# One layer kernel with three mixers: decay rates moved within the first stage, and attention's products with the values issued for two key blocks and both heads together

## The chip, the cores and the metric

The kernel runs on one core of a Trainium2 chip. A core has five engines with a queue of instructions each: TensorE (PE in the profile; its weight loads are PEld), VectorE (DVE), ScalarE (ACT), GpSimd (POOL) and SyncE (SP, which only issues transfers here). The metric is the device time of one execution in microseconds. The kernel before takes 876.51 us, the median of three runs (876.1 to 877.89).

## The reference, cut to what matters

Two layers work on 512 tokens of width 1024, all in 32-bit floats. Each layer normalises its input, projects it, runs three mixers side by side on the projection, and adds their gated and projected outputs to its input.

```python
for l in range(DEPTH):                      # DEPTH = 2
    xn = rms_norm(h, ln_g[l])
    proj = xn @ w_in[l]
    u_a, z_a, u_b, z_b, q_lat, kv_lat, k_rope, z_c = jnp.split(proj, pts, axis=-1)
    y_a = rwkv7_mix(u_a, ...)               # a recurrence over tokens, 8 heads of 64
    y_b = rms_norm(rglru_mix(u_b, ..., lru_lam[l]), lru_out_g[l])
    y_c = rms_norm(mla_mix(q_lat, kv_lat, k_rope, ...), mla_out_g[l])
    y = concatenate([y_a * silu(z_a), y_b * silu(z_b), y_c * silu(z_c)])
    h = h + y @ w_out[l]
return rms_norm(h, final_g)
```

Two pieces matter here. In `rglru_mix` the decay of the gated recurrence is `log_a = -8 * gate_r * softplus(-lam)`. The factor `softplus(-lam)` depends on the parameter `lam` alone (512 numbers in each layer). In `mla_mix` each of 8 heads computes causal attention: scores, a softmax over the keys up to the query, and the product of the probabilities with the values, in blocks of 128 queries and keys.

```python
s = jnp.where(k_pos[None, :] <= q_pos[:, None], s, -jnp.inf)
p = jax.nn.softmax(s, axis=-1).astype(v.dtype)
return jnp.einsum('bhqk,bkhd->bqhd', p, v)
```

## The kernel before, in words

Tiles have 128 partitions. The large projections are made of three products each (`mm3`, L230 to L233), with weight and activation split into a high and a low part; ScalarE makes the high part of a weight (L140 through `copy`), GpSimd or VectorE the low part (L227).

A layer runs in stages. Orders written by hand name the steps of the first stages: ORD1 for the recurrence's inputs, then ORD2 and ORD3. In ORD1, `M` is the projection and token mix of a head pair (L498 is VectorE's share), `L` the low-rank products with a sigmoid on ScalarE (L540, L541), `C` the chain that forms decay, keys and their scaling (L552 to L584, mostly on VectorE, with exponentials on ScalarE and products on GpSimd), `O` a bonus term (L592 to L595), `P` the products of keys with queries and their masks (L610 on TensorE, L613 on VectorE, then transposes L628), and `U` the values (L637). Four head pairs are numbered 0 to 3. ORD2 begins with gates (`G`), the remaining `U` and `P`, and the substitution `X` (L728 to L749), a long run of VectorE instructions behind which the corner products L758 to L773 stand.

The program order gives each instruction its priority. A planner in the framework then fixes each engine's queue ahead of time: it takes the ready instruction of the highest priority by its own costs, adds the waits that the data need, and the hardware works each queue in order. Activation functions that need a table are chained in program order on ScalarE (`act`, L132).

`decay_rates` (L260 to L278) computes the softplus of both layers once, in layer one, after ORD1. It is one exponential on ScalarE and 25 VectorE instructions on 128 x 8 numbers, among them a polynomial in a loop (L271 to L273). Its results, `sp8` and `nsp8`, are read by the gated recurrence (L694, L701).

Attention works on head pairs too. `score_steps` gives 8 steps for each pair: a score product (L1037) into one of four accumulators, a mask and a maximum on VectorE (L1038, L1039), the exponential with its sum on ScalarE (L1041, by way of L137), and the scaling on VectorE (L1044). `heads` then takes the four key blocks one after the other: for both heads it transposes the probabilities (L1056), copies them to SBUF on ScalarE (L1058, shown as L140), runs fill steps, and multiplies by the values (L1062). The stationary operand there is 128 x 64, and each product is two passes on TensorE. Head 0 writes partitions 0 to 63 of `ot`, head 1 partitions 64 to 127. The fill steps come from the string QH: `s` is a score step of the next head pair, `u` a step of the output projection (L405 is its sum on VectorE).

## Time and profile before

| What | Value |
| --- | --- |
| Median of three runs | 876.51 us (876.1 to 877.89) |
| Profiled execution | 874.73 us, its span 873.0 us |
| Mean granted TensorE clock | 0.973 |
| TensorE busy | 810.8 us, 93% of the span |
| VectorE busy | 578.5 us, 66% |
| ScalarE busy | 494.3 us, 57% |
| GpSimd busy | 336.5 us, 39% |

In the profile a group of instructions is named by line, engine and operation, with the tile written, an arrow and the tiles read. In a timeline the first number is the start in microseconds from the begin of the span and the second the time until the last of the merged instructions ended; a bracket gives the idle time before the first and what ended it. Since matmuls are pipelined, their times overlap, and the distance from start to start is what one costs. A line of `copy`, `act` or `mm3` stands for all who call it.

### The profile page before, as it was taken

The numbers are of one execution on the slowest core, as the hardware profiler recorded it, in microseconds if no ns is written. First come the engines' busy times: TensorE is split into PE (matmuls) and PEld (weight loads), VectorE is DVE, ScalarE is ACT, GpSimd is POOL, SyncE is SP. The second block draws the span as 40 slices with busy tenths as digits, with TensorE's granted clock in tenths as the row PEclk, the third lists the DMA queues.
The fourth block names the chain that finished last, engine by engine and source line by source line (L and its number), as shares of the span: only waits on it lengthen the run. The fifth ranks groups of instructions, "written<-read, shape, count | busy, mean of one in ns | idle before, by whom it ended". The sixth has DMA issues, their size and how long they took to land.

```text
span 873.0 us, 14713 instructions
## 1 busy us (share of the span) xinstructions
PE 810.8 (93%) x5440; PEld 621.4 (71%) x5440; DVE 578.5 (66%) x1176; ACT 494.3 (57%) x980; POOL 336.5 (39%) x303
## 2 busy tenths in 40 slices
PE   3999997998989988999989999999989998899995
PEld 2878886876768866655778788888756886665574
DVE  5678777843656795974484766786265777677636
ACT  5667874457454535564466677844645445465635
POOL 2355554634343342010534655665243423310223
PEclk9999997999899999999989999999999999999998
DMA  6322232420212365222653222333010224731354
GB/s 217 115 73 71 72 103 84 139 74 13 56 39 72 106 221 182 73 68 98 206 195 97 73 93 88 100 107 115 27 42 23 65 86 154 227 114 49 108 168 159
DMA packets 49753, 91.05 MB, mean 104 GB/s; under 512 B 5520, under 2 KB 8336, under 8 KB 49680
## 3 DMA queue, kind: packets, MB, share of 16 engines
q1 hardware_dynamic: 49104, 89.05, 31.7%
q10 hardware_dynamic: 576, 1.05, 0.3%
q8 instruction: 43, 0.70, 0.3%
q14 instruction: 30, 0.25, 0.1%
HBM read 73.30 MB, written 16.78 MB: 103 GB/s over the span
## 4 chain that ended last, share of the span: by engine, by line
PE 69%; DVE 14%; DMA 5%; ACT 5%; issue 4%; POOL 2%; SPq 0%; ACTq 0%; DVEq 0%; POOLq 0%
PE acc L231 15%; PE acc L233 15%; PE acc L232 15%; PE acc L1037 4%; PE ck L1062 3%; PE ps L1056 3%; PE ps L688 2%; PE ck L829 2%; ACT g L137 2%; DMA dr<-hp 2%; DMA g<-dr 1%; POOL g L703 1%; PE ps L628 1%; PE ps L610 1%; PE ck L788 1%
## 5 line engine op out<-in xcount | busy, mean ns | idle before, releaser
L227 POOL TENSOR_TENSOR wL<-wr,wH 128x512 fp32r<-128x512 f32 (+1 forms) x130 | 176.8, 1365 | 291.8 <-ACT wH L140 271.3
L140 ACT ACTIVATE wH<-wr 128x512 fp32r<-128x512 f32 (+1 forms) x192 | 118.7, 622 | 135.7 <-PE acc L232 77.5
L231 PE MATMUL acc<-xH,wH 128*128 128x512 f32 (+1 forms) x496 | 193.0, 390 | 0.0
L233 PE MATMUL acc<-xH,wL 128*128 128x512 f32 (+1 forms) x496 | 192.0, 387 | 0.0
L232 PE MATMUL acc<-xL,wH 128*128 128x512 f32 (+1 forms) x496 | 190.4, 384 | 0.5 <-DVE xL L305 0.4
L231 PEld LDWEIGHTS acc<-xH,wH 128*128 128x128 f32 x496 | 95.5, 193 | 20.8 <-issue 3.2
L232 PEld LDWEIGHTS acc<-xL,wH 128*128 128x128 f32 x496 | 95.7, 193 | 17.9 <-DVE xL L305 1.2
L233 PEld LDWEIGHTS acc<-xH,wL 128*128 128x128 f32 x496 | 95.5, 192 | 17.8
L231 PE MATMUL acc<-wH,c 128*128 128x512 f32 x192 | 81.9, 426 | 4.3 <-DVE hp L427 4.3
L227 DVE TENSOR_TENSOR wL<-wr,wH 128x512 fp32r<-128x512 f32 (+1 forms) x62 | 51.5, 830 | 48.7 <-ACT wH L140 48.6
L232 PE MATMUL acc<-wL,c 128*128 128x512 f32 x192 | 76.8, 400 | 0.4 <-DVE wL L227 0.4
L233 PE MATMUL acc<-wH,c 128*128 128x512 f32 x192 | 76.3, 399 | 0.0
L140 ACT ACTIVATE UV<-ps 128x512 f32<-128x512 f32 (+4 forms) x88 | 39.0, 477 | 38.0 <-PE ps L1056 30.6
L231 PEld LDWEIGHTS acc<-wH,c 128*128 128x128 f32 x192 | 36.3, 189 | 16.1 <-DVE hp L427 3.2
L137 ACT ACTIVATE g<-g 128x512 f32<-128x512 f32 (+1 forms) x58 | 36.5, 628 | 17.5 <-DVE g L706 15.6
L137 ACT ACTIVATE c<-acc,sm 128x128 f32<-128x128 f32 (+3 forms) x64 | 33.6, 527 | 18.7 <-DVE sm L1039 18.5
L233 PEld LDWEIGHTS acc<-wH,c 128*128 128x128 f32 x192 | 36.3, 189 | 8.6 <-issue 1.0
L140 ACT ACTIVATE c<-g 128x512 fp32r<-128x512 f32 (+1 forms) x40 | 24.3, 628 | 31.9 <-DVE g L960 26.4
L232 PEld LDWEIGHTS acc<-wL,c 128*128 128x128 f32 x192 | 36.5, 190 | 8.2 <-issue 1.4
L1037 PE MATMUL acc<-am,am 128*128 128x128 f32 (+3 forms) x128 | 41.5, 445 | 0.8 <-ACT c L137 0.8
L368 POOL TENSOR_TENSOR g<-g,g 128x512 f32<-128x512 f32 x24 | 33.4, 1394 | 12.6 <-ACT g L137 12.6
L135 ACT ACT_TABLE_LOAD x29 | 37.2, 1283 | 1.2 <-PEq L1189 0.7
(218 smaller groups left out, 1604.5 us busy)
## 6 DMA issues: line engine op xcount, KB each, us to landing
wr<-in_wc_dram SPq DMA_DIRECT2D x116, 256.0 KB, 2.7
wr<-in_wo_dram SPq DMA_DIRECT2D x48, 256.0 KB, 3.5
hp<-dr SPq DMA_DIRECT2D x40, 256.0 KB, 3.1
dr<-hp SPq DMA_DIRECT2D x32, 256.0 KB, 2.8
dr<-g SPq DMA_DIRECT2D x16, 256.0 KB, 2.3
g<-dr SPq DMA_DIRECT2D x16, 256.0 KB, 3.6
wr<-in_wl_dram SPq DMA_DIRECT2D x16, 208.0 KB, 2.4
c<-in_x_dram SPq DMA_DIRECT2D x8, 256.0 KB, 6.5
```

Source lines behind the costliest of these rows:

```text
L135: chained(A.preload_act_table_set(SETS[st]))
L137: chained(A.activation(out=out, in_=in_, func=func, **kw))
L140: i = A.activation(out=out, in_=in_, func=AF.Copy, **kw)
L227: (V if wn[0] % wmod[0] == 0 else G).tensor_tensor(out=L, in0=raw, in1=f(H), op=ALU.subtract)
L231: PE.matmul(o, a[0], b[0], start=start, stop=False)
L232: PE.matmul(o, a[0], b[1], start=False, stop=False)
L233: PE.matmul(o, a[1], b[0], start=False, stop=stop)
L368: G.tensor_tensor(out=z, in0=z, in1=s, op=ALU.mult)
L688: PE.matmul(o[hr, :], gw[hr, w, j, :], xc[hr, :], start=True, stop=True)
L1037: PE.matmul(o[:, 0:n], qT[:, hd, qt * 128:n], K2[:, p, e, 0:n], start=True, stop=True)
L1056: PE.transpose(o[:, (qt - kt) * 128:(qt - kt + 1) * 128], Pm[p][e, qt][:, kt * 128:(kt + 1) * 128], ident)
L1062: PE.matmul(ot[e * 64:(e + 1) * 64, kt * 128:T], Vt[:, kt, 2 * p + e, :], pts[e][:, 0:n], start=(kt == 0), stop=(kt == 3))
```

## The change

There are two parts. First, `decay_rates` becomes a step `D` of ORD1, behind the low-rank products `L0` and `L1` and ahead of the first chain `C0`, in layer one only. Its polynomial is also written with fused instructions, which add a constant and multiply in one: 18 VectorE instructions stand in place of 25.

Second, in `heads` the products with the values are issued after each second key block. The group holds both heads of the earlier block and both heads of the later one. Its first product gets an added dependency on the last of the copies of the later block. The fill steps keep their places, behind each block's copies.

```diff
-    ORD1 = "M0 L0 L1 C0 M1 C1 P0 L2 O0 M2 U1 O1 C2 U2 P1 L3 M3 C3 U0 P2 O2"
+    ORD1 = "M0 L0 L1 D0 C0 M1 C1 P0 L2 O0 M2 U1 O1 C2 U2 P1 L3 M3 C3 U0 P2 O2"
...
+    SYNC = mybir.DependencyInfo(mybir.DependencyClass.Sync, mybir.DependencyReason.DATA)
...
-        V.tensor_scalar(out=l3, in0=l2, scalar1=1.0 / 17.0, scalar2=1.0 / 15.0, op0=ALU.mult, op1=ALU.add)
-        for n in (13, 11, 9, 7, 5, 3, 1):
-            V.tensor_tensor(out=l3, in0=l3, in1=l2, op=ALU.mult)
-            V.tensor_scalar(out=l3, in0=l3, scalar1=1.0 / n, scalar2=None, op0=ALU.add)
-        V.tensor_tensor(out=l3, in0=l3, in1=l1, op=ALU.mult)
+        V.tensor_scalar(out=l3, in0=l2, scalar1=1.0 / 17.0, scalar2=None, op0=ALU.mult)
+        for n in (15, 13, 11, 9, 7, 5, 3):
+            V.scalar_tensor_tensor(out=l3, in0=l3, scalar=1.0 / n, in1=l2, op0=ALU.add, op1=ALU.mult)
+        V.scalar_tensor_tensor(out=l3, in0=l3, scalar=1.0, in1=l1, op0=ALU.add, op1=ALU.mult)
...
-        steps = {"L": low_rank, "M": mixes, "C": chain, "O": bonus_term, "P": products, "U": values}
+        steps = {"D": lambda _: decay_rates() if l == 0 else None, "L": low_rank, "M": mixes, "C": chain, "O": bonus_term, "P": products, "U": values}
...
-        if l == 0:
-            decay_rates()
...
-                pts = []
                 for e in range(2):
                     o = ps()
                     for qt in range(kt, 4):
                         PE.transpose(...)
-                    pt = PT[:, 2 * (kt % 2) + e, :]
-                    copy(pt[:, 0:n], o[:, 0:n])
-                    pts.append(pt)
+                    last_pt = copy(PT[:, 2 * (kt % 2) + e, 0:n], o[:, 0:n])
                 fill[kt]()
-                for e in range(2):
-                    PE.matmul(ot[e * 64:(e + 1) * 64, kt * 128:T], Vt[:, kt, 2 * p + e, :], pts[e][:, 0:n], start=(kt == 0), stop=(kt == 3))
+                if kt % 2 == 0:
+                    continue
+                for k2 in (kt - 1, kt):
+                    for e in range(2):
+                        i = PE.matmul(ot[e * 64:(e + 1) * 64, k2 * 128:T], Vt[:, k2, 2 * p + e, :], PT[:, 2 * (k2 % 2) + e, 0:(4 - k2) * 128],
+                                      start=(k2 == 0), stop=(k2 == 3))
+                        if k2 < kt and e == 0:
+                            tc.add_manual_dep(i.ins, last_pt.name, SYNC, reason="one group")
```

## The prediction

> **What bounds the kernel now.** I read the page first, then the chain of waits, then windows and timelines of the two places that the edits touch. TensorE is busy nearly all the time and carries most of the chain, so a change counts by what it does to TensorE's queue: its idle stretches, its clock, and the length of its own instructions.

> ```profile
> span 873.0 us, 14713 instructions
> ...
> PE 810.8 (93%) x5440; PEld 621.4 (71%) x5440; DVE 578.5 (66%) x1176; ACT 494.3 (57%) x980; POOL 336.5 (39%) x303
> ...
> PE 69%; DVE 14%; DMA 5%; ACT 5%; issue 4%; POOL 2%; SPq 0%; ACTq 0%; DVEq 0%; POOLq 0%
> ```

> The profiled execution took 874.73 us, 1.78 us below the median of the runs (876.51). The sum is made against 874.73 and 1.8 is added at the end.

> Both layers run the same stages, and only layer one has the decay rates. So layer two serves as a measurement of layer one without them. The chain of waits gives two marks in each layer: a group of the key-value products and the first corner product after the substitution.

> ```profile
> 94.45 1.16 PE ps L610 x8
> ...
> 180.68 1.91 PE ck L758 x64
> ...
> 524.86 1.16 PE ps L610 x8
> ...
> 602.86 1.91 PE ck L758 x64
> ```

> Layer one takes 180.68 - 94.45 = 86.23 us, layer two 602.86 - 524.86 = 78.00: layer one is 8.2 us longer over the same work. The windows show where (columns: busy time and count of TensorE, weight loads, VectorE, ScalarE, GpSimd, then the granted clock, the DMA share and GB/s):

> ```profile
> 134.10:139.30 5.20, 0.23 (x3) 0.04 (x1) 4.79 (x16) 0.27 (x1) 2.23 (x2) 0.67 0.63 200
> 139.30:146.20 6.90, 6.88 (x23) 5.73 (x24) 2.57 (x4) 3.78 (x6) 0.00 (x0) 0.51 0.00 1
> ```

> TensorE stands still for 5 us while VectorE runs 16 instructions, and then works 6.9 us at a granted clock of 0.51. The idle time costs 5.2, the clock 6.9 x (1 - 0.51) = 3.4; together 8.6, near the 8.2 of the marks. In layer two:

> ```profile
> 564.50:569.70 5.20, 5.20 (x31) 4.28 (x31) 2.61 (x5) 3.98 (x8) 1.82 (x2) 1.00 0.58 186
> ```

> TensorE is full in the same 5.2 us and the clock is 1.00. What VectorE does in layer one's gap, and who waits (timelines of VectorE and TensorE):

> ```profile
> 131.30 1.25 DVE L273 TENSOR_SCALAR sm<-sm 128x8 f32<-128x8 f32 x1
> ...
> 136.40 0.17 DVE L272 TENSOR_TENSOR sm<-sm,sm 128x8 f32<-128x8 f32 x1
> ...
> 138.58 0.68 DVE L613 TENSOR_TENSOR am<-ps,C 128x512 f32<-128x512 f32 x1
> ```
> ```profile
> 139.32 1.11 PE L628 MATMUL ps<-C,c 128*128 128x128 f32 x4 [4.99 <-DVE am L613]
> ```

> The decay polynomial (L272, L273 and what follows) stands in VectorE's queue ahead of the mask products L613 of the third head pair; TensorE waits 4.99 us for them.

> **The change part by part: the decay rates.** The chain has 25 VectorE instructions before and 18 after (14 instructions of the loop become 7, the rest as before). Two of the 18 read only the inputs, which leaves 16 in a row behind the exponential. Moved behind layer one's first two low-rank products, they are no longer ahead of L613. What is late next there is nothing that layer two's windows show, so I take the whole 8.2 as gained. No DMA is issued by this step, and no table load is added: the exponential's table is loaded at that place anyway, before the first chain's exponential.

> Their new place costs something. ScalarE runs the exponential behind this table load, and VectorE has a hole there (timelines of ScalarE, VectorE and GpSimd):

> ```profile
> 49.45 1.28 ACT L135 ACT_TABLE_LOAD   x1
> ```
> ```profile
> 53.63 0.82 DVE L567 TENSOR_TENSOR c<-g 128x512 f32<-128x512 f32 x1 [3.05 <-ACT g L137]
> ```
> ```profile
> 51.45 1.20 POOL L579 TENSOR_TENSOR c<-g,g 128x512 f32<-128x512 f32 x1 [3.74 <-ACT g L137]
> ...
> 54.20 1.40 POOL L227 TENSOR_TENSOR wL<-wr,wH 128x512 fp32r<-128x512 f32 x1 [0.29 <-ACT wH L140]
> ```

> Lower bound: 16 x 0.17 = 2.7 us inside a hole of 3.05, so 0; they only add work, so there is no gain below nothing. Upper bound: the first of the loop's instructions show durations of 1.25 beside 0.17. From 131.30 to 136.40 there are five of them in 5.1 us. GpSimd worked through that stretch until its last instruction ended at 136.33, and from then on the same instruction took 0.17:

> ```profile
> 135.07 1.26 POOL L368 TENSOR_TENSOR g<-g,g 128x512 f32<-128x512 f32 x1
> ```

> At the new place GpSimd is busy from 51.45 to 55.60 almost without a break. About 2 instructions get through before 51.45, 5 until 55.60, and the other 9 at 0.2 end near 57.4: L567 and the first chain behind it start 3.8 us late. Queued behind them on VectorE are L567 to L592 and the mask products of the first head pair, for which TensorE waits. How much of a delay reaches TensorE is read from this window:

> ```profile
> 54.00:68.00 14.00, 13.05 (x71) 10.37 (x70) 12.44 (x16) 7.34 (x15) 9.29 (x10) 1.00 0.23 76
> ```

> VectorE has 14.00 - 12.44 = 1.6 us idle in it, so 3.8 - 1.6 = 2.2 us get through. Bounds 0 and 3.8; I take 2.2, since five equal instructions of this kernel beside a busy GpSimd are the nearest row. Net of this edit: 8.2 - 2.2 = 6.0 us (4.4 to 8.2).

> [...]

> **The change part by part: attention's products with the values.** Before, the products of one key block (two heads, each in two passes) follow that block's transposes; after, two blocks and both heads stand together, and the first waits for the last of the four copies. TensorE's timeline:

> ```profile
> 367.99 0.87 PE L1062 MATMUL ck<-UV 128*64 128x384 f32 x4
> 368.79 0.66 PE L1056 MATMUL ps<-C,c 128*128 128x128 f32 x4
> ...
> 371.13 0.40 PE L233 MATMUL acc<-wH,c 128*128 128x512 f32 x1
> 371.45 0.65 PE L1062 MATMUL ck<-UV 128*64 128x256 f32 x4
> 372.04 0.44 PE L1056 MATMUL ps<-C,c 128*128 128x128 f32 x2
> ...
> 372.54 0.40 PE L232 MATMUL acc<-wL,c 128*128 128x512 f32 x1
> 372.78 0.40 PE L233 MATMUL acc<-wH,c 128*128 128x512 f32 x1
> ...
> 376.06 1.07 PE L1062 MATMUL ck<-UV 128*64 128x512 f32 x2
> 377.07 0.70 PE L1037 MATMUL acc<-am,am 128*128 128x256 f32 x2
> 377.70 1.07 PE L1062 MATMUL ck<-UV 128*64 128x512 f32 x2
> ...
> 397.88 0.86 PE L1062 MATMUL ck<-UV 128*64 128x384 f32 x2
> 398.67 0.50 PE L231 MATMUL acc<-wH,c 128*128 128x512 f32 x1
> ```

> Read from start to next start: a pair of both heads (x4) takes 0.59 at 256 columns and 0.80 at 384, and one head alone (x2) takes 0.79 at 384 and 1.01 at 512. So the second head is free when it stands beside the first, each 128 columns cost 0.21, and 0.16 is left over (0.59 - 2 x 0.21) that is paid once at the end of each group. On the way in, 371.13 to 371.45 is 0.32, where 372.54 to 372.78 is 0.24: 0.08 more, also once for each group.

> Merging: 4 head pairs x 4 blocks x 2 layers make 32 groups into 16. Saved: 16 x (0.16 + 0.08) = 3.8 us. No TensorE instruction goes away.

> Split pairs: at 376.06 the first head goes alone, a score product (L1037) gets between, and the second head pays the whole again: 1.01 + 0.08 = 1.09. The same stands in the third head pair, and there 384 columns are split too (397.88, with an output product between): 0.79 + 0.08 = 0.87. In the first pair the second head came late:

> ```profile
> 361.92 1.51 PE L1062 MATMUL ck<-UV 128*64 128x512 f32 x4
> 363.36 0.87 PE L1056 MATMUL ps<-C,c 128*128 128x128 f32 x6
> ```

> 1.44 in place of 1.01, so 0.43. One layer: 2 x 1.09 + 0.87 + 0.43 = 3.5. The windows of one head pair in both layers agree to the hundredth, so the other layer has the same:

> ```profile
> 376.06:391.43 15.37, 15.37 (x71) 8.53 (x71) 11.40 (x36) 10.31 (x31) 3.38 (x3) 1.00 0.15 48
> ...
> 798.63:814.00 15.37, 15.37 (x72) 8.54 (x71) 11.41 (x36) 10.31 (x31) 3.39 (x3) 1.00 0.15 53
> ```

> That is 7.0 us at most. With all four copies awaited, the four products become ready together, but a fill step that stands ahead of them in program order and becomes ready meanwhile may still be put between. Bounds 0 and 7.0; I take two thirds, 4.7, because the long score products have mostly left when the group comes. TensorE is full in these windows and VectorE has 15.37 - 11.40 = 4.0 us to spare for each head pair, so TensorE's saving becomes time. The transposes of the second block no longer have products ahead of them, but they need only the copies that those products awaited too. The slots of the transposed probabilities are rewritten by copies that follow transposes standing behind the group in TensorE's queue: no new wait. Attention: 3.8 + 4.7 = 8.5 (3.8 to 10.8).

> Sum: 6.0 + 8.5 = 14.5; 874.7 - 14.5 = 860.2; against the median 862.0. By the bounds: gains of 4.4 + 3.8 = 8.2 to 8.2 + 10.8 = 19.0, so 868.3 to 857.5.

> **Rivals.** (1) The first chain is late by all 3.8 us and the gap that this opens on TensorE lowers its clock. Rows of a gap of nearly that size, the wait (between 250 and 258) and the window behind it:

> ```profile
> PE ck L822 <- ACT c L865: 2.7, 1, 2.7
> ```
> ```profile
> 255.00:258.00 3.00, 2.73 (x21) 2.55 (x22) 3.00 (x3) 0.70 (x2) 1.98 (x2) 0.56 0.32 85
> ```

> Price 3.8 + 3.4 (the clock's loss above) = 7.2, which leaves 1.0 of the decay's gain: 876.5 - 1.0 - 8.5 = 867.0. For it: VectorE is 89% busy in 54 to 68. Against: TensorE has projections to run there. [...]

> (2) Fill steps split the new groups as they split the pairs: only the merging is left, 6.0 + 3.8 = 9.8, 866.7. For it: in the rows above both a score product and an output product got between.

> (3) The change doesn't hold its group together: only the first product has the added wait, and the other head's product of the first block could be taken alone as soon as its own copy is done. Then 8 groups pay 1.09 and 8 pay 0.59 + 0.08 = 0.67 again, 14.1 us, against 10.8: attention loses 3.3, the decay keeps 6.0, 873.8. Against: in the rows, pairs otherwise go in order.

> (4) Slower: the first group of each head pair waits on ScalarE. Its last copy stands in ScalarE's order among the exponentials, and these wait for VectorE:

> ```profile
> 381.83 0.19 ACT L137 ACTIVATION_READ_ACCUMULATOR c<-acc,sm 128x1 f32 x1
> 382.74 0.58 ACT L137 ACTIVATE c<-acc,sm 128x384 f32<-128x384 f32 x1 [0.71 <-DVE sm L1039]
> ```

> Two such exponentials ahead of the copy are 2 x (0.71 + 0.58 + 0.19) = 3.0 us of standstill, in 8 groups 23.7: 876.5 + 23.7 - 14.5 = 885.7. It turns the sign from 14.5 / 8 = 1.8 us a group. For it: everything behind the group in TensorE's queue waits too. Against: the second block's four scores and one output step cover the copies.

> **How the numbers follow.** The forecast has 0.60, rivals (1) 0.10, (2) 0.14, (3) 0.07, (4) 0.09. What a measurement here can tell from no change is about 0.2%, 1.8 us. Faster takes the first three cases and most of (3): 0.86; no change 0.05, the rest of (3) and mild forms of (4); slower 0.09. The predicted time is 862, the range 856 to 872: the bounds, widened by 1.5 below for an order that falls out better, and above to cover (1), (2) and part of (3).

> **What would show it.** Right: no wait of TensorE's L628 for L613 over 1 us in layer one, the clock at 1.00 behind it, and the stretch between the two marks near 78 us; the decay's instructions near 51 to 57 us; 16 groups of products with the values, of 8 passes, some 1.6 us (0.21 x 7 + 0.16) and 0.8 us (0.21 x 3 + 0.16) long. Wrong: a new gap on TensorE near 60 to 68; groups of fewer than 8 passes; waits of L1062 on copies above 1 us; the stretch still 86 us long.

## The result and the profile after

The kernel after takes 871.79 us, the median of seven runs (867.09 to 874.36), against 876.10 for seven of the kernel before. The ratio is 0.9941 with a 95% interval of 0.9923 to 0.9958: 5.2 us faster, between 3.7 and 6.7. (The gains in this document are those of the ratios; the two medians alone lie 4.3 us apart, which is within the interval.) The sign is as forecast, and the time lies inside the range, near its slow end, but the gain is little more than a third of the 14.5 us that the sum gave. The profiled execution took 871.72 us. Lines from 123 on have moved by one in `copy`, `act` and `mm3` (L231 to L233 are now L232 to L234, L140 is L141), and in attention the scores are L1035, the transposes L1053 and the products with the values L1061. TensorE is as full as before, 808.5 us or 93% of the span.

The marks of the prediction, from the chain of waits (a group of key-value products and the first corner product, once in each layer):

```profile
101.27 1.16 PE ps L610 x8
...
179.30 1.91 PE ck L756 x64
...
521.56 1.16 PE ps L610 x8
...
599.56 1.92 PE ck L756 x64
```

Between its marks layer one now takes 179.30 - 101.27 = 78.03 us, layer two 78.00. The 8.2 us that layer one was longer are gone, as forecast. But the first mark itself stands at 101.27 in place of 94.45: 6.8 us were lost ahead of it. That is the first place to look at. VectorE there, in the kernel after:

```profile
50.98 0.17 DVE L267 TENSOR_SCALAR sm<-sm 128x8 f32<-128x8 f32 x1 [0.40 <-ACT sm L138]
...
51.62 1.15 DVE L270 TENSOR_TENSOR sm<-sm 128x8 f32<-128x8 f32 x1
52.80 1.23 DVE L271 TENSOR_SCALAR sm<-sm 128x8 f32<-128x8 f32 x1
54.07 2.36 DVE L273 SCALAR_TENSOR_TENSOR sm<-sm,sm 128x8 f32<-128x8 f32 x7
...
57.02 0.68 DVE L567 TENSOR_TENSOR c<-g 128x512 f32<-128x512 f32 x1
57.73 0.69 DVE L568 SCALAR_TENSOR_TENSOR c<-c,c 128x512 f32<-128x512 f32 x1
58.34 0.74 DVE L498 SCALAR_TENSOR_TENSOR g<-acc,omu,hp 128x512 f32<-128x512 f32 x1
```

The rates fill 50.98 to 57.1, and L567 of the first chain starts at 57.02 instead of 53.63, 3.4 us late. Two instructions further on the delay is smaller. The same rows in the kernel before:

```profile
54.49 1.66 DVE L568 SCALAR_TENSOR_TENSOR c<-c,c 128x512 f32<-128x512 f32 x1
56.07 0.74 DVE L498 SCALAR_TENSOR_TENSOR g<-acc,omu,hp 128x512 f32<-128x512 f32 x1
```

L498 is 58.34 - 56.07 = 2.27 us late, because L567 and L568 now take 0.68 and 0.69 us where they took 0.82 and 1.66: in the kernel before, GpSimd was still busy beside them (until 55.60), and now it is done by then. From there the 2.27 us stay as they are. TensorE, before (the first two rows) and after:

```profile
64.13 0.39 PE L233 MATMUL acc<-xH,wL 128*128 128x512 f32 x1
64.89 0.49 PE L524 MATMUL ps<-c,bones 128*128 128x512 f32 x1 [0.38 <-ACT c L140]
```
```profile
64.12 0.39 PE L234 MATMUL acc<-xH,wL 128*128 128x512 f32 x1
67.16 0.50 PE L524 MATMUL ps<-c,bones 128*128 128x512 f32 x1 [2.65 <-ACT c L141]
```

Behind the last projection TensorE now waits 2.65 us in place of 0.38 for the key norms of the second chain, so the next product comes 67.16 - 64.89 = 2.27 us late. The other 4.5 us of the 6.8 are lost while the clock is at half. The windows below (time, length, then busy time and count of TensorE, weight loads, VectorE, ScalarE and GpSimd, then the granted clock, the DMA share and GB/s) are cut where the clock changes; of the kernel after:

```profile
66.07:69.48 3.41, 1.77 (x16) 1.23 (x18) 2.01 (x4) 3.30 (x7) 3.41 (x5) 1.00 0.22 77
69.48:72.90 3.42, 3.42 (x19) 2.87 (x17) 3.00 (x5) 3.38 (x6) 2.26 (x4) 0.50 0.47 152
72.90:76.31 3.41, 3.41 (x14) 3.09 (x15) 1.65 (x4) 1.91 (x4) 0.00 (x0) 0.50 0.00 1
76.31:79.72 3.41, 3.41 (x9) 2.64 (x9) 3.20 (x6) 0.51 (x1) 0.00 (x0) 0.50 0.00 0
```

TensorE is full from 69.48 to 79.72 and runs at half clock all that time; before, the clock was 1.00 there. At the old place, in 134 to 139 us, the clock is now 1.00 and TensorE is full. So the moved step gained 8.2 and lost 6.8.

Second place: attention. TensorE in the kernel after, the first head pair's two groups and the second pair's first:

```profile
365.43 1.07 PE L1061 MATMUL ck<-UV 128*64 128x512 f32 x2
366.44 0.50 PE L232 MATMUL acc<-wH,c 128*128 128x512 f32 x1
...
367.34 1.72 PE L1061 MATMUL ck<-UV 128*64 128x512 f32 x6
...
372.35 0.87 PE L1061 MATMUL ck<-UV 128*64 128x256 f32 x8
...
379.27 1.07 PE L1061 MATMUL ck<-UV 128*64 128x512 f32 x2
380.27 1.98 PE L1035 MATMUL acc<-am,am 128*128 128x512 f32 x4
382.19 1.72 PE L1061 MATMUL ck<-UV 128*64 128x512 f32 x6
```

The second group of a head pair is whole: eight passes, 0.80 us from its start to the next one. Of the first group the first product (two passes) stands alone for 1.0 us, then come an output step or score products, and then the other six passes take 1.65 us, as long as eight are meant to. The third head pair shows the same, the fourth not, and layer two repeats layer one: six splits are left.

The stage as a whole, from its first score product to the first product of the token sums (L378), before and then after:

```profile
351.02 1.26 PE L1037 MATMUL acc<-am,am 128*128 128x128 f32 x6
...
423.92 0.95 PE L378 MATMUL ck<-ones,sqn 128*128 128x2 f32 x8
```
```profile
350.11 1.64 PE L1035 MATMUL acc<-am,am 128*128 128x128 f32 x8
...
421.18 0.95 PE L378 MATMUL ck<-ones,sqn 128*128 128x2 f32 x8
```

That is 72.90 us before and 71.07 after. In layer two it is 72.68 and 71.07. Attention gained 1.8 + 1.6 = 3.4 us in all.

The two sums, 1.4 and 3.4, make 4.8; the two profiled executions are 3.0 apart. The missing 1.8 were lost between 600 and 772 us, where the change touches nothing. Behind one and the same kind of wait, for L427 on VectorE (2.4 us before, 3.1 after), the clock is at half for one window of 3.41 us before (757.10 to 760.51) and for two after (752.15 to 758.97); over all of 600 to 772 us there are three such windows before and four after. I take this for chance of the single execution, for the reason in the last section, and have not shown it; it is why the experiments below are read stage by stage from the traces and only then by their times.

### The profile page after: what moved, and what is told of

The parts are those of the page before. It is cut to its first block, busy times and chain, and to the rows that moved or that the text cites. A ratio compares the mean times of both kernels' runs of the same rounds, so it can differ in the third digit from the quotient of the medians.

```text
span 869.9 us, 14682 instructions
## 1 busy us (share of the span) xinstructions
PE 808.5 (93%) x5440; PEld 624.9 (72%) x5440; DVE 575.0 (66%) x1169; ACT 493.7 (57%) x980; POOL 336.1 (39%) x303
## 4 chain that ended last, share of the span: by engine, by line
PE 70%; DVE 12%; ACT 6%; DMA 4%; issue 4%; POOL 2%; SPq 0%; ACTq 0%; DVEq 0%; POOLq 0%
PE acc L232 16%; PE acc L234 15%; PE acc L233 15%; PE acc L1035 4%; PE ck L1061 3%; PE ps L1053 2%; ACT g L138 2%; PE ps L686 2%; PE ck L827 2%; PE ps L610 1%; ACT UV L141 1%; PE ps L628 1%; DMA dr<-hp 1%; POOL g L701 1%; DMA hp<-in_x_dram 1%
## 5 line engine op out<-in xcount | busy, mean ns | idle before, releaser
L141 ACT ACTIVATE wH<-wr 128x512 fp32r<-128x512 f32 (+1 forms) x192 | 118.9, 622 | 138.9 <-PE acc L233 81.0
L232 PE MATMUL acc<-xH,wH 128*128 128x512 f32 (+1 forms) x496 | 193.5, 391 | 0.0
L234 PE MATMUL acc<-xH,wL 128*128 128x512 f32 (+1 forms) x496 | 192.1, 387 | 0.0
L233 PE MATMUL acc<-xL,wH 128*128 128x512 f32 (+1 forms) x496 | 190.4, 384 | 0.1
L232 PEld LDWEIGHTS acc<-xH,wH 128*128 128x128 f32 x496 | 95.7, 193 | 20.8 <-issue 3.2
L233 PEld LDWEIGHTS acc<-xL,wH 128*128 128x128 f32 x496 | 95.7, 193 | 17.5 <-DVE xL L305 0.6
L234 PEld LDWEIGHTS acc<-xH,wL 128*128 128x128 f32 x496 | 95.3, 192 | 18.0
L232 PE MATMUL acc<-wH,c 128*128 128x512 f32 x192 | 82.7, 431 | 4.2 <-DVE hp L427 4.2
L233 PE MATMUL acc<-wL,c 128*128 128x512 f32 x192 | 77.1, 402 | 0.2 <-DVE wL L228 0.2
L234 PE MATMUL acc<-wH,c 128*128 128x512 f32 x192 | 76.4, 400 | 0.0
L141 ACT ACTIVATE UV<-ps 128x512 f32<-128x512 f32 (+4 forms) x88 | 39.3, 478 | 31.0 <-PE ps L1053 22.4
L232 PEld LDWEIGHTS acc<-wH,c 128*128 128x128 f32 x192 | 36.4, 190 | 15.2 <-ACT c L141 3.0
L1035 PE MATMUL acc<-am,am 128*128 128x128 f32 (+3 forms) x128 | 42.3, 447 | 0.9 <-ACT c L138 0.8
L233 PEld LDWEIGHTS acc<-wL,c 128*128 128x128 f32 x192 | 36.6, 191 | 8.3 <-issue 1.4
L234 PEld LDWEIGHTS acc<-wH,c 128*128 128x128 f32 x192 | 36.5, 190 | 8.4 <-issue 0.5
L141 ACT ACTIVATE c<-g 128x512 fp32r<-128x512 f32 (+1 forms) x40 | 24.3, 628 | 28.9 <-DVE g L958 26.0
L368 POOL TENSOR_TENSOR g<-g,g 128x512 f32<-128x512 f32 x24 | 33.0, 1377 | 12.5 <-ACT g L138 12.5
```

The source lines that it names most:

```text
L141: i = A.activation(out=out, in_=in_, func=AF.Copy, **kw)
L232: PE.matmul(o, a[0], b[0], start=start, stop=False)
L233: PE.matmul(o, a[0], b[1], start=False, stop=False)
L234: PE.matmul(o, a[1], b[0], start=False, stop=stop)
L368: G.tensor_tensor(out=z, in0=z, in1=s, op=ALU.mult)
L1035: PE.matmul(o[:, 0:n], qT[:, hd, qt * 128:n], K2[:, p, e, 0:n], start=True, stop=True)
```

## The experiments

Theory A: the moved rates cost nearly all that they gain because the wait of TensorE at 64 us halves its clock, and attention keeps its splits because fill steps get between the first product of a group and the rest. Theory B, the rival: the two parts are worth what the sum says (6.0 and 8.5), and one takes from the other, or something outside both costs time. Each kernel is the kernel before with the edit shown, unless the text says otherwise, and each ratio is to the kernel before in runs on the same chip.

**e1, the rates alone.** All of the change's edits to `decay_rates` and ORD1, attention as before:

```diff
+    ORD1 = "M0 L0 L1 D0 C0 M1 C1 P0 L2 O0 M2 U1 O1 C2 U2 P1 L3 M3 C3 U0 P2 O2"
```

> Only the decay rates are moved and fused; attention as before. Theory A (the rates at their new place delay layer one's first chain, TensorE falls idle for some 2.7 us near 65 us, and its clock is halved behind that, so that 6.8 of the 8.2 us are lost again): 1.0 to 2.5 us faster than before, the clock near 0.5 between 70 and 79 us. Theory B (the rates bring their 6 us, and attention's grouping gives some back): 5 to 7 us faster.

Measured: 0.9974 (0.9949 to 0.9999), 2.3 us faster. The profiled execution was the slowest of the twelve (881.58 us, the median 874.28), so only its first stages are read here. TensorE and the mark, from its timeline and chain:

```profile
63.47 0.39 PE L233 MATMUL acc<-xH,wL 128*128 128x512 f32 x1
66.50 0.49 PE L523 MATMUL ps<-c,bones 128*128 128x512 f32 x1 [2.65 <-ACT c L140]
```
```profile
100.59 1.16 PE ps L609 x8
...
178.60 1.91 PE ck L755 x64
```

The same wait of 2.65 us; from the last projection to the mark it takes 100.59 - 63.47 = 37.12 us, where it takes 94.45 - 64.13 = 30.32 in the kernel before: 6.8 lost. Behind the mark the stretch is 78.01. The rates account for their part alone, without the other edit.

**e2, attention alone.** The other half of the change, the rates as before:

```diff
+                if kt % 2 == 0:
+                    continue
+                for k2 in (kt - 1, kt):
...
+                            tc.add_manual_dep(i.ins, last_pt.name, SYNC, reason="one group")
```

> Only attention's products are grouped; the decay rates as before. Theory A (grouping saves 3.3 us, since three of the four first groups of each layer are split again): 2.5 to 4.5 us faster. Theory B: no faster, up to 2 us slower. By the prediction's own term it would be 8.5 us faster.

Measured: 0.9949 (0.9929 to 0.9968), 4.5 us faster. Its attention stages last 71.07 and 71.05 us, with the splits at the same places. The parts do not disturb each other: 2.3 + 4.5 = 6.8, and the whole change has 5.2 (3.7 to 6.7) with intervals of about 2 on each part. Neither part alone is worth what theory B says, 6.0 and 8.5.

**e3, no rates at all.** What would the first part be worth at best?

```diff
     def decay_rates():
-        lam = vecs[:, :, VO["lam"]:VO["lam"] + 4]
...
+        G.memset(sp8, 0.5)
+        G.memset(nsp8, -0.5)
```

> Attention as before; the computation of the decay rates is left out, two constants are written by GpSimd in its place (the gated recurrence then decays at a wrong rate). This is the most that any new place of the rates can bring. Theory A: 7.5 to 9 us faster than before, TensorE without the wait of 5 us near 134 us, the clock 1.00 there and near 65 us. If the wait near 134 us had another cause behind it (the products of the third head pair late for their own reasons): under 4 us faster.

Measured: 0.9899 (0.9876 to 0.9921), 8.9 us faster. No wait at 134 us, the clock at 1.00, no half clock in the first stage. The 8.2 of the marks was the right size for the old place.

**e8, the fused polynomial at the old place.** It separates the fewer instructions from the move:

```diff
-        for n in (13, 11, 9, 7, 5, 3, 1):
-            V.tensor_tensor(out=l3, in0=l3, in1=l2, op=ALU.mult)
-            V.tensor_scalar(out=l3, in0=l3, scalar1=1.0 / n, scalar2=None, op0=ALU.add)
+        for n in (15, 13, 11, 9, 7, 5, 3):
+            V.scalar_tensor_tensor(out=l3, in0=l3, scalar=1.0 / n, in1=l2, op0=ALU.add, op1=ALU.mult)
```

> The polynomial is fused (18 instructions in place of 25) but stays behind the first stage; attention as before. By the durations of the trace before, 7 of some 21 instructions less ahead of the masks: TensorE's wait near 134 us falls from 5.0 to between 2 and 4 us, and the clock behind it is still lowered: 1.5 to 4 us faster than before. If the wait falls far enough that the clock stays at 1.00: 5 to 7 us faster.

Measured: 0.9972 (0.996 to 0.9984), 2.5 us faster.

```profile
138.56 1.12 PE L627 MATMUL ps<-C,c 128*128 128x128 f32 x4 [3.56 <-DVE am L612]
```
```profile
138.16:141.57 3.41, 3.01 (x12) 2.50 (x12) 1.54 (x3) 1.88 (x3) 0.00 (x0) 0.50 0.17 65
```

The wait shrinks from 4.99 to 3.56 us and still halves the clock. Fusing alone is worth as much as the whole first part of the change: moving the fused step on top of that gained nothing that can be measured (e1 2.3, e8 2.5).

**e6, a shorter step at the new place.** As e1 with three of the seven steps of the polynomial (the rates come out less exact), to see how the loss goes with the length of the wait:

```diff
-        for n in (15, 13, 11, 9, 7, 5, 3):
+        for n in (7, 5, 3):
```

> The decay rates moved as in the change, attention as before; the polynomial keeps 3 of its 7 steps (the rates come out less exact), so VectorE is held some 0.8 us less ahead of the first chain. If the larger part of the loss is the halved clock, and a gap of some 1.8 us does not halve it: 5 us faster than with the whole polynomial, 6 to 8 us faster than before, the clock 1.00 in 68 to 80 us. If the loss grows with the delay alone, or if 1.8 us halve the clock too: 0.8 us faster than with the whole polynomial, 2 to 4 us faster than before.

Measured: 0.9952 (0.9937 to 0.9968), 4.2 us faster.

```profile
66.75 0.49 PE L523 MATMUL ps<-c,bones 128*128 128x512 f32 x1 [1.84 <-ACT c L140]
```
```profile
65.69:69.10 3.41, 1.79 (x16) 1.24 (x18) 2.02 (x4) 3.28 (x7) 3.41 (x5) 1.00 0.25 77
69.10:72.52 3.42, 3.42 (x19) 2.86 (x16) 3.02 (x5) 3.38 (x6) 2.24 (x4) 0.50 0.58 152
```

A wait of 1.84 us is enough for the same three windows at half clock (69.10 to 79.34). My expectation that a wait of this length would spare the clock is wrong.

**e9 and e10, the wait filled with products that nobody needs.** VectorE, ScalarE and GpSimd are as in e1; only TensorE is given something to do while it waits, ten or six products into an accumulator that is overwritten afterwards:

```diff
+            for _ in range(fill):
+                i = PE.matmul(o, bones, w2[:, 0, :], start=True, stop=True)
+                tc.add_manual_dep(i.ins, last_pe[0].ins.name, NOSYNC, reason="in the gap")
             PE.matmul(o, bones, H, start=True, stop=False)
```

> This is e1 (rates moved, attention as before) with ten products that nobody needs put into the 2.65-us gap on TensorE: they stand behind the last projection of the second head pair, write the accumulator of the head sums that follow, and are overwritten by them. VectorE, ScalarE and GpSimd have the same work as in e1, so TensorE's own instructions are as late as there. Theory A (the idle time itself lowers the clock): ten products of 0.23 us leave about 0.4 us of the gap, the clock stays at 1.00 between 68 and 80 us, and the 4.5 us behind the gap are not lost: 2.3 + 4.5 = 6.8 us faster than before, ratio near 0.992. Theory B (the clock falls for another reason, such as the mix of work of that stretch or the length of the chain): the clock is still 0.50 there and the time is that of e1, 2.3 us faster than before, ratio near 0.997.

Measured: 0.9937 (0.9915 to 0.9959), 5.5 us faster. TensorE, the window and the mark of e9:

```profile
64.30 0.39 PE L234 MATMUL acc<-xH,wL 128*128 128x512 f32 x1
64.53 2.46 PE L525 MATMUL ps<-c,bones 128*128 128x512 f32 x10
67.34 0.51 PE L527 MATMUL ps<-c,bones 128*128 128x512 f32 x1 [0.36 <-ACT c L140]
...
73.14 1.04 PE L613 MATMUL ck<-c,c 64*128 64x128 f32 x7 [0.83 <-DVE am L616]
```
```profile
66.03:69.44 3.41, 2.48 (x17) 1.40 (x17) 2.58 (x4) 3.38 (x7) 3.41 (x4) 1.00 0.24 77
```
```profile
98.06 1.16 PE ps L613 x8
```

The clock stays at 1.00. The key norms come as late as in e1, but the mark now stands 98.06 - 64.30 = 33.76 us behind the last projection, 3.4 later than in the kernel before instead of 6.8. So the half clock was worth 3.4 us of e1's time and not all of 4.5: with TensorE at full speed another wait shows, 0.83 us for VectorE at 73.14, which the slow clock had hidden.

> As e9 with six products in place of ten: about 2.65 - 6 x 0.23 = 1.3 us of the gap stay open. Theory A with a limit between 0.6 and 1.84 us: which side of it 1.3 us lies on is what the run tells. If the clock is 1.00 between 68 and 80 us, the time is that of e9, ratio near 0.992; if it falls to about 0.5, the time is that of e1, near 0.997. Theory B: as e1 in any case.

Measured: 0.9972 (0.9954 to 0.999), 2.5 us faster, as e1; its mark stands 37.4 us behind the last projection. A wait of 1.28 us stays open, and the clock falls:

```profile
65.95:69.36 3.41, 1.71 (x16) 1.17 (x18) 2.58 (x4) 3.38 (x8) 3.41 (x5) 1.00 0.24 77
69.36:72.77 3.41, 3.41 (x21) 3.19 (x18) 2.74 (x5) 3.21 (x5) 2.31 (x4) 0.50 0.49 147
```

Useless work brought 3 us (3.4 by the marks of e1 and e9), and it is only TensorE's idle time that differs between e1, e10 and e9: it is the cause of the half clock. TensorE was busy for 1.71 of 3.41 us in the window ahead of the fall here, and for 2.48 in e9.

**e4, the rates in a hole.** The exponential moves to the start, behind the first norm, and the fused polynomial into a hole of VectorE ahead of the first low-rank products:

```diff
+            with tc.issue_after(getattr(last_split, "ins", last_split)):
+                decay_series()
...
+    decay_rates()
     for l in range(depth):
         one_layer(l)
```

> Attention as before; the exponential stands right behind the first normalisation, and the fused polynomial behind the split of layer one's low-rank input, where VectorE is idle from 37.4 to 40.7 us. Theory A (it is the place that loses the gain): 7 to 9 us faster than before, no idle time of TensorE above 1 us between 30 and 140 us. Rival (VectorE has no time to spare anywhere ahead of the first chain, so any place there costs it): 1 to 4 us faster, with a gap of TensorE near 65 us again.

Measured: 0.9897 (0.9873 to 0.9922), 9.0 us faster. VectorE and TensorE of e4:

```profile
37.00 1.05 DVE L273 TENSOR_SCALAR sm<-sm 128x8 f32<-128x8 f32 x1
...
39.73 1.37 DVE L279 SCALAR_TENSOR_TENSOR sm<-sm,sm 128x8 f32<-128x8 f32 x7
```
```profile
64.55 0.49 PE L530 MATMUL ps<-c,bones 128*128 128x512 f32 x1 [0.36 <-ACT c L140]
```

The step now starts at 37.00 and its loop ends at 39.73 + 1.37 = 41.10, and TensorE's wait at 64 is 0.36 us, as before the change. This gives all that e3 gives by leaving the rates out. So the place was the fault, and a good one exists.

**e5, attention with the group held behind its fill steps.** As e2, and the first product of each group also stands behind the last score product and the last output product that were issued:

```diff
                             tc.add_manual_dep(i.ins, last_pt.name, SYNC, reason="one group")
+                            for q in last_pe:
+                                tc.add_manual_dep(i.ins, q.ins.name, NOSYNC, reason="behind the fill")
```

> Attention's part alone, and the first product of each group is also queued behind the last score step and the last output step of its fill, so that no fill step can stand inside a group; the decay rates as in the kernel before. Theory A (what the grouping did not bring is the split of six first groups, 1.0 us each): about 6 us faster than the grouping alone, 9 to 11 us faster than before. Rival (the fill steps that stood inside the groups now make TensorE wait for VectorE's maxima or for a free accumulator, so the time moves into waits of the score products or of the groups): within 2 us of the grouping alone, that is 2.5 to 6.5 us faster than before, with new waits of TensorE on ScalarE or VectorE in 350 to 420 us.

Measured: 0.9873 (0.9852 to 0.9893), 11.1 us faster. The first head pair's two groups, and the two ends of the stage:

```profile
368.23 1.73 PE L1065 MATMUL ck<-UV 128*64 128x512 f32 x8
...
373.09 0.87 PE L1065 MATMUL ck<-UV 128*64 128x256 f32 x8
```
```profile
351.97 0.27 PE L1039 MATMUL acc<-am,am 128*128 128x128 f32 x1
...
419.63 0.95 PE L380 MATMUL ck<-ones,sqn 128*128 128x2 f32 x8
```

All sixteen groups have eight passes. The stage lasts 67.66 us, 3.4 less than in the kernel after, and 67.67 in layer two: the splits cost 6.8 us in all. No wait of TensorE above 0.4 us is new in these stages, so holding the groups back costs nothing there.

**e7, both mended.** e4 and e5 in one kernel.

> The polynomial in VectorE's hole and the groups of attention behind their fill, together. If both mends hold and don't meet: the sum of the two, 9 + 10 = 19 us faster than before. If the groups behind their fill bring nothing more than the grouping alone: 12 to 14 us faster.

Measured: 859.22 us, 0.981 (0.9791 to 0.983): 16.7 us faster than before, the fastest kernel here. Its attention stages last 68.16 us, 0.5 longer each than in e5. The rest of the difference to the sum of the parts, 9.0 + 11.1 = 20.1, lies within the intervals, and was not followed further.

## Why the prediction was right in sign and wrong in size

**What bounds the kernel, and the 8.2 us.** Right. TensorE's full stretches turn what they save into time, and the rates' old place cost what the marks of the two layers said (8.9 by e3, 78.03 us between the marks after).

**The term of the new place, "2.2 us get through".** Its number came out nearly to the tenth, but by luck. L567 was 3.4 us late where 3.8 had been forecast: only three of the small instructions took over a microsecond (1.15, 1.23 and 1.15 us), not five, and in the row that served as the model it was four and one of 0.17. TensorE was 2.27 late where 2.2 had been forecast, but not because VectorE's 1.6 us of idle time took up the rest. The delay fell from 3.4 to 2.27 at L567 and L568, which ran faster later, and VectorE's idle time behind them took up nothing: its wait for ScalarE ahead of L210 (L211 after) is 0.80 us before and 0.81 after.

The step that failed is that the sum stopped at this wait. "Net of this edit: 8.2 - 2.2 = 6.0" left the clock out, though a row shown for rival (1), a 2.7-us wait with a clock of 0.56 behind it, had nearly the size of the wait that the sum itself forecast. The term measured 6.8 us, and the edit is worth 1.4 by the traces (2.3 by e1's times). By e9 it would have been 3.4 us even at full clock, since a second wait for VectorE stands behind the first; the half clock cost the other 3.4.

Rival (1) had the price (7.2) and tied it to a delay "by all 3.8 us"; the delay that I took as likeliest was already enough: with a wait of 2.65 us TensorE was busy for 1.77 of the 3.41 us from 66.07 to 69.48, and the clock fell to 0.50 behind them. Its chance of 0.10 was the error. That a delay of 2.2 us would leave the clock alone was not shown by any row. The row of rival (1) spoke against it: TensorE's wait was 2.7 us there, it was busy for 0.70 of the 3.41 us ahead of the fall (251.94 to 255.35), and the clock was 0.56 in 255 to 258.

**Merging, 3.8.** Right, as far as it can be told apart: the two stages gained 3.4 in all, and nearly nothing of that is healed splits (below). Groups of eight passes last 1.66 us (368.23 to 369.89 in e5) and 0.80, where 1.63 and 0.79 were worked out.

**Healed split pairs, "two thirds, 4.7".** This is the second step that failed. The first three head pairs of both layers still have a split, and by e5 these cost 6.8 us where 7.0 had been forecast for all: about 0.2 was healed. My reason, that "the long score products have mostly left when the group comes", is not what decides. As I read it, the planner issues the group's first product as soon as the last copy is done by its own costs, and by the time the next one could go, a fill step, which stands ahead in program order, has become ready and takes its turn. The traces show the fill step in that place, and e5 shows that an order behind the fill removes the split; the planner's own steps are not on record. That is rival (2), word for word, at 0.14.

**The rivals together.** Each of them was worked out with the other term at its full forecast, and no case had both. By their own prices both together give 876.5 - (8.2 - 7.2) - 3.8 = 871.7 us; measured 871.8. Rivals (3) and (4) did not come: no group falls apart further than its first product, and the groups wait for no copy, as the groups by shape show for the longest of the kernel after (busy time, mean ns, idle time ahead):

```profile
L1061 PE MATMUL ck<-UV 128*64 128x512 f32 x32 | 15.0, 618 | 0.0
```

**What was named as a sign.** "A new gap on TensorE near 60 to 68" and "groups of fewer than 8 passes" both came true, as signs of being wrong.

## What to carry to other kernels

When a step is moved, ask of the engine that sets the time not only how long it will wait but in what share of a few microseconds it will be idle, and price the clock with it: here TensorE's idle time in 48% of 3.41 us was followed by half clock, and 2.3 us of waiting cost 6.8. A wait for the last input does not hold a group of instructions together when other ready work stands ahead of it in priority; put the group's first instruction behind that work, or it will be split at the same places as before. And when two rivals each rest on a different term, work out the time with both.

## What the runs showed of the hardware

Two things follow from these counts, as estimates. If the limit is put at half a window, an idle time of between 1.7 and 3.4 us halves the clock or spares it by where it falls on the grid, so the same kernel can lose a different number of windows in each execution, about 1.7 us each where TensorE is full. That would fit the 7 us over which the seven times of the kernel after spread, and its extra window near 755 us; neither was tested by itself. The clocks on record fit it too: of the seven executions the fastest (867.09 us) had a mean granted clock of 0.983 and the slowest (874.36) 0.969, and of the twelve of e1 the fastest (869.36) 0.982 and the slowest (881.58) 0.969. And a half-clock window costs less than 1.7 us where other engines were late anyway: with the wait of 0.83 us at 73.14 in e9, the three windows of e1 cost 3.4 us, 1.1 each.

How the clock comes back stayed open. No window at half clock in which TensorE was busy for under 85% ended with full clock (10 of them), but of 57 busier ones 11 did not either, among them the two between 69.48 and 76.31 us in the kernel after, where TensorE is busy throughout. They hold the products of 64 rows (L610, until 74.70). What kept the clock at 0.50 there was not tried.

VectorE beside GpSimd: each of the three small instructions that took 1.15 to 1.23 us instead of 0.17 in the kernel after ended within 0.04 us of the end of one of GpSimd's three instructions there (52.74, 54.00 and 55.60). The four slow ones at the old place in the kernel before ended in the same way (132.53, 133.89, 135.11 and 136.33). So in these two stretches there was one slow instruction of VectorE for each instruction of GpSimd that it met.
